# Scores of 24 expert chunks made ahead in the query and gate stages and kept in DRAM; the gathered tokens' slots chosen inside the first V group; six row places

## The chip, the cores and the metric

The kernel runs on one core of a Trainium2 chip. A core has five engines that run their own instruction queues and wait for each other with semaphores: PE (TensorE: matmuls), DVE (VectorE), ACT (ScalarE), POOL (GpSimd) and SP (SyncE, which here only starts DMAs). The metric is the time of one execution on the device, in microseconds; lower is better. The time before is the median of three runs.

## The reference

One step of a one-layer decoder: attention with a sliding window next to a gated linear recurrence, an output projection, and then the part that takes most of the time, a layer of 16,384 experts (PEER). For each of 576 tokens and each of 8 heads it finds the 16 best experts by two sets of 128 keys, and adds up their outputs:

```python
q = (hc @ w_pq).reshape(c, PEER_HEADS, 2, D_KEY // 2)
s = jnp.einsum('nhcd,hckd->nhck', q, sub_keys).astype(jnp.float32)
sv, si = lax.top_k(s, PEER_TOPK)
cand = (sv[:, :, 0, :, None] + sv[:, :, 1, None, :]).reshape(c, PEER_HEADS, -1)
cid = (si[:, :, 0, :, None] * N_KEYS + si[:, :, 1, None, :]).reshape(c, PEER_HEADS, -1)
best, pos = lax.top_k(cand, PEER_TOPK)
eid = jnp.take_along_axis(cid, pos, axis=-1)
g = jax.nn.softmax(best, axis=-1)
act = jax.nn.gelu(jnp.einsum('nd,nhkd->nhk', hc, peer_u[eid]).astype(jnp.float32))
return jnp.einsum('nhk,nhkd->nd', (g * act).astype(hc.dtype), peer_v[eid])
```

D_MODEL is 2048, PEER_HEADS 8, PEER_TOPK 16, N_KEYS 128; peer_u and peer_v are 16,384 x 2,048 in float32.

## The kernel before

**The tokens.** 416 tokens ("dense") go through all 16,384 experts: their scores against every row of u, times a gate that is zero for experts not chosen, times v. The other 160 tokens ("gathered") have the rows of their chosen experts fetched one by one with indirect DMAs. Both go on at once.

**Pieces.** Every weight comes in pieces of 256 KB: SP starts the load (`raw`), ACT copies it to `phi` (the high part, line 89), and DVE or POOL subtracts to get `plo` (the low part, line 90). `mm3` (lines 93 to 96) multiplies with three matmuls, high by high, high by low and low by high. The raw buffers are 3, and 4 more (`rawx`) once a pool is put into the list `deep`.

**Stages.** Projections, attention and recurrence, and the output projection (0 to 721 us of the trace). Then:
- *Query stage*: 8 heads. For each head PE makes the queries (`pdq` for the dense tokens and 32 of the others, `pgq` for 128 gathered tokens) and the scores `psc` against the keys; DVE and POOL choose the top 16 (`head_top`, `tile_ids`). The 128 gathered tokens' queries go to DRAM (`qgd`).
- *Gate stage* (lines 925 to 968): 13 groups of 32 tokens, 4 blocks of 8 each. DVE builds two one-hot factors `ohA` and `ohB`, PE multiplies them to the gates `pgg` of these tokens over all experts (8 matmuls in float32, 16 records in the trace), ACT copies them into `stg`, and SP writes the group to DRAM (`Gd`), since in SBUF there is no room for all.
- *Main loop*: 16 groups of 8 chunks, a chunk being 128 experts. `u_chunk` makes the scores of one chunk for the dense tokens (`sps`: 4 pieces, 48 matmuls of 416 columns), scales them and applies GELU (`e`). `w_chunk` multiplies `e` with the chunk's gates, read back from `Gd` (`gs`), and splits the product into `wth` and `wtl`. `v_group` multiplies a group's 8 weights with V: 16 output blocks `po` of 24 matmuls and two pieces each, which DVE adds into `acc`.
- *Gathered rows*: 640 jobs, each an indirect DMA of a half row of u or v (on POOL's queue, into one of four places `row`) and one DVE instruction on it. `pace` hands them out, so many for each "unit" (half a chunk or one output block), from unit 40 on. Before the first, `gather_top` has to choose the experts of the 128 gathered tokens: 8 heads of scores (`psg_`) and top 16, then the numbers.

**What sets the order.** The code is written in one order, and a scheduler orders each engine's queue by what it thinks is ready; it also moves work across stages as far as buffers allow. The scores of the first 8 chunks are kept in 8 buffers `ep`, so that chunks 0 to 4 run while DVE finishes the last head (the "tail") and chunks 5 to 7 are held by `g_late` until the last but one block of gates, to lie beside the way of the gates through DRAM (the "round trip"). `gather_top` stands between them and V group 0 in the code.

Of the kernel before, what the change touches and what calls it, by code (L numbers as in the profile page):

```python
# [35 lines left out]
EB = 8  # L36
# [3 lines left out]
UNIT0 = 40  # L40
# [4 lines left out]
def tile_hymba_peer_step(ctx: ExitStack, tc: tile.TileContext, a, o, dbg=None):  # L45
# [78 lines left out]
    Gd = gd_pool.tile([NSG, P, NGRP, 8, GRP], F32, name="Gd")  # L124

# [588 lines left out]
    def ffn_rstd():  # L714
# [104 lines left out]
    with tc.tile_pool(name="tq", bufs=1) as tq:  # L819
# [34 lines left out]

        for h in range(8):
# [42 lines left out]
    epx = ctx.enter_context(ExitStack())  # L898
    ep = [epx.enter_context(tc.tile_pool(name="ep", bufs=EB, side="right"))]


    psx = ctx.enter_context(tc.tile_pool(name="psx", bufs=2, space=PSUM))
    with tc.tile_pool(name="gb", bufs=1) as gbp, tc.tile_pool(name="psg", bufs=2, space=PSUM) as psg:
# [31 lines left out]

        nxt = prep(0)
        fac = factors(*nxt, 0)
        for r in range(NGRP):
# [8 lines left out]
            for q in range(GRP // BT):  # L947
# [25 lines left out]
    GT = ctx.enter_context(tc.tile_pool(name="gt", bufs=1))  # L973
# [6 lines left out]
    def row():  # L980
        return mn.tile([P, 1024], F32, tag="row", name="row", bufs=4)

    def gather_top():
# [25 lines left out]
        dve.tensor_scalar(idx2[:, 1], t1, 2.0, 1.0, op0=ALU.mult, op1=ALU.add)  # L1009

# [83 lines left out]
    es = {}  # L1094

    def u_chunk(c):

        sps = psx.tile([P, DEN], F32, name="sps")
        for q in range(4):
            held = EB - 3 <= c < 8  # L1100
            wh, wl, ins = piece(a["uT"][c, :, q * 4:q * 4 + 4], [P, 4, P], c < 8 and q % 2 == 1)
            with tc.issue_after(g_late.ins) if held else nullcontext():
                for d in range(4):
                    dk = q * 4 + d
                    mm3(sps, wh[:, d], wl[:, d], uh[dk][:, 0:DEN], ul[dk][:, 0:DEN], dk == 0, dk == NK - 1)
            if q % 2 == 1:
                pace(ins)
        e = ep[0].tile([P, DEN], F32, name="e")
        dve.tensor_tensor(e, sps, rd[:, 0:DEN], op=ALU.mult)
        act.activation(e, e, AF.Gelu_apprx_tanh)  # L1110
# [159 lines left out]
```

## Time and profile before

| what | us |
|---|---|
| median of three runs | 3446.27 |
| the three runs | 3442.35, 3447.62, 3446.27 |
| profiled execution, its own time | 3442.77 |
| its span in the trace | 3440.9 |
| query stage | 721 to 958 |
| tail | 958 to 1013 |
| gate stage | 1013 to 1151 |
| round trip | 1151 to 1202 |
| V groups and U chunks | 1202 to 3437 |

The stages' limits are read from the timeline of PE and DVE: 721 is the first `pdq`, 958 about where the last scores `psc` are done, 1013 the first `pgg`, 1151 the end of the last one, 1202 about the first `po`. A busy PE is one that works on a matmul; its clock can be lower than full, which the column PEclk tells (1.00 is full speed).

### The profile page before, as it was taken

Reading aid. Unit: us, or ns where it says so; the run is one execution under the profiler, and the core shown is the slowest. Engines: PE = TensorE matmul, PEld = TensorE weight load, DVE = VectorE, ACT = ScalarE, POOL = GpSimd, SP = SyncE. Lnnn points to the kernel's source line nnn. Section 1 sums busy time; section 2 is a strip of 40 time slices with the busy share of each in tenths; the row PEclk is TensorE's granted clock in tenths of the full one; section 3 lists DMA queues with packets and bytes.
Section 4 is the critical chain, followed back from the end, with each engine's and each line's share of the span. In section 5 each row is a group of like instructions: output and inputs, shape, how many; then the busy total and the mean of one; then the engine's idle time right before and its main releaser. Section 6 shows DMA issues by size and latency. Waiting matters only on the chain.

```text
span 3440.9 us, 52423 instructions
## 1 busy us (share of the span) xinstructions
PE 3358.9 (98%) x18611; PEld 3222.1 (94%) x18611; DVE 2550.5 (74%) x4765; ACT 1228.3 (36%) x2119; POOL 1200.3 (35%) x1174
## 2 busy tenths in 40 slices
PE   9999999999987899999999999999999999999999
PEld 7888888899887799999999999999999999999999
DVE  5386755446989777778787787877777778787786
ACT  4245533333233333333233332333333333333332
POOL 6562321124730123333333333333333333333331
PEclk9999999999999999999999999999999999999999
DMA  4211223433235647888888888888888888888886
GB/s 146 83 62 58 64 68 113 122 108 90 75 103 196 205 154 271 279 296 275 296 292 280 297 276 296 292 281 298 276 296 288 281 295 289 308 291 280 293 281 211
DMA packets 352774, 753.67 MB, mean 219 GB/s; under 512 B 39904, under 2 KB 104032, under 8 KB 352224
## 3 DMA queue, kind: packets, MB, share of 16 engines
q1 hardware_dynamic: 260352, 414.73, 35.4%
q0 software_dynamic: 92160, 335.59, 29.9%
q8 instruction: 147, 2.41, 0.3%
q14 instruction: 115, 0.94, 0.1%
HBM read 715.51 MB, written 36.59 MB: 219 GB/s over the span
## 4 chain that ended last, share of the span: by engine, by line
PE 84%; DVE 10%; POOL 2%; issue 1%; DMA 1%; ACT 1%; SPq 0%; POOLq 0%; ACTq 0%; DVEq 0%
PE po L96 11%; PE po L94 11%; PE po L95 11%; PE sps L94 11%; PE sps L95 11%; PE sps L96 11%; PE pd L96 2%; PE pd L95 2%; DVE ohA L952 2%; PE pd L94 2%; PE zp L94 1%; PE zp L95 1%; PE zp L96 1%; DVE ohB L954 1%; PE mm L94 1%
## 5 line engine op out<-in xcount | busy, mean ns | idle before, releaser
L89 ACT ACTIVATE phi<-raw 128x512 fp32r<-128x512 f32 x1200 | 757.0, 632 | 1693.8 <-PE po L95 747.1
L90 DVE TENSOR_TENSOR plo<-raw,phi 128x512 fp32r<-128x512 f32 x1132 | 796.6, 704 | 288.0 <-ACT phi L89 280.4
L96 PE MATMUL po<-wth,plo 128*128 128x416 f32 x2048 | 722.4, 353 | 0.6 <-DVE plo L90 0.6
L94 PE MATMUL po<-wth,phi 128*128 128x416 f32 x2048 | 717.7, 351 | 0.3 <-DVE acc L1137 0.3
L95 PE MATMUL po<-wtl,phi 128*128 128x416 f32 x2048 | 715.0, 349 | 0.0
L1013 POOL DMA_INDIRECT row<-in_u,idx x320 | 372.3, 1164 | 712.8 <-DVE au L1019 600.1
L1013 POOL DMA_INDIRECT row<-in_v,idx x320 | 383.5, 1198 | 669.9 <-DVE xg L1025 447.0
L96 PE MATMUL sps<-uha,plo 128*128 128x416 f32 x1536 | 538.0, 350 | 7.2 <-DVE plo L90 7.2
L94 PE MATMUL sps<-uha,phi 128*128 128x416 f32 x1536 | 537.7, 350 | 6.1 <-ACT phi L89 5.5
L95 PE MATMUL sps<-ula,phi 128*128 128x416 f32 x1536 | 537.2, 350 | 0.0
L95 PEld LDWEIGHTS po<-wtl,phi 128*128 128x128 f32 x2048 | 384.7, 188 | 5.9
L96 PEld LDWEIGHTS po<-wth,plo 128*128 128x128 f32 x2048 | 384.0, 188 | 3.4 <-DVE plo L90 0.9
L94 PEld LDWEIGHTS po<-wth,phi 128*128 128x128 f32 x2048 | 384.4, 188 | 2.8 <-DVE acc L1137 0.7
L1025 DVE SCALAR_TENSOR_TENSOR xg<-row,gg,xg 128x1024 f32<-128x1024 f32 x256 | 321.9, 1279 | 0.1
L1019 DVE CUSTOM_DVE_ANT_0 row<-row,hg 128x1024 f32<-128x1024 f32 x256 | 307.0, 1218 | 0.1
L96 PEld LDWEIGHTS sps<-uha,plo 128*128 128x128 f32 x1536 | 289.1, 188 | 9.3 <-DVE plo L90 9.2
L94 PEld LDWEIGHTS sps<-uha,phi 128*128 128x128 f32 x1536 | 289.1, 188 | 7.2 <-ACT phi L89 6.2
L95 PEld LDWEIGHTS sps<-ula,phi 128*128 128x128 f32 x1536 | 289.1, 188 | 0.1
L1137 DVE TENSOR_TENSOR acc<-po,acc 128x416 f32<-128x416 f32 x256 | 150.9, 590 | 182.9 <-PE po L96 182.8
L90 POOL TENSOR_TENSOR plo<-raw,phi 128x512 fp32r<-128x512 f32 x68 | 94.3, 1389 | 269.9 <-ACT phi L89 260.2
L96 PE MATMUL sps<-uhb,plo 128*128 128x416 f32 x512 | 180.2, 352 | 0.8 <-POOL plo L90 0.7
L94 PE MATMUL sps<-uhb,phi 128*128 128x416 f32 x512 | 180.2, 352 | 0.5 <-ACT phi L89 0.5
(427 smaller groups left out, 5401.2 us busy)
## 6 DMA issues: line engine op xcount, KB each, us to landing
raw<-in_uT SPq DMA_DIRECT2D x512, 256.0 KB
raw<-in_vL SPq DMA_DIRECT2D x512, 256.0 KB
Gd<-stg SPq DMA_DIRECT2D x13, 2048.0 KB
gs<-Gd SPq DMA_DIRECT2D x196, 128.0 KB
raw<-in_wlru SPq DMA_DIRECT2D x64, 256.0 KB
raw<-in_wout SPq DMA_DIRECT2D x64, 256.0 KB
raw<-in_wpq SPq DMA_DIRECT2D x64, 256.0 KB
raw<-in_wqkv SPq DMA_DIRECT2D x48, 256.0 KB
```

Source lines behind the costliest of these rows:

```text
L89: act.activation(hi, raw, AF.Copy)
L90: ins = (pool if on_pool else dve).tensor_tensor(lo, raw, hi.bitcast(F32), op=ALU.subtract)
L94: pe.matmul(out, lhsT=sh, rhs=mh, start=first, stop=False)
L95: pe.matmul(out, lhsT=sh, rhs=ml, start=False, stop=False)
L96: pe.matmul(out, lhsT=sl, rhs=mh, start=False, stop=last)
L952: dve.tensor_tensor(ohA, oa[:, q0, :, None].to_broadcast([P, BT, 16, 8]), ob[:, q0, None, :].to_broadcast([P, BT, 16, 8]), op=ALU.mult)
L954: dve.tensor_tensor(ohB, tT[:, 1, n0:n0 + BT, None].to_broadcast([P, BT, P]), iot[:, None, :].to_broadcast([P, BT, P]), op=ALU.is_equal)
L1013: pool.indirect_dma_start(out=r, out_offset=None, in_=uv[w], in_offset=bass.IndirectOffsetOnAxis(ap=idx2[:, half, e:e + 1], axis=0))
L1019: dve.tensor_tensor_reduce(r, r, rows[0][:, half * 1024:half * 1024 + 1024], 1.0, 0.0, ALU.mult, ALU.add, au[:, half, e:e + 1])
L1025: dve.scalar_tensor_tensor(xs, r, gg[:, e:e + 1], xs, op0=ALU.mult, op1=ALU.add)
L1137: dve.tensor_tensor(acc[:, b, 0:DEN], po, acc[:, b, 0:DEN], op=ALU.add)
```

## The change

- `u_chunk` becomes `u_parts`, a generator that makes a chunk's scores piece by piece. In the query stage one chunk follows each head (chunks 0 to 7; the odd pieces' `plo` on POOL). In the gate stage a generator `ahead` gives out the 64 pieces of chunks 8 to 23 evenly over the 52 blocks, all `plo` on DVE.
- The scores of chunks 0 to 39 go from SBUF to DRAM tiles `Ed` with a DMA on ACT's queue, and `w_chunk` reads them back with a DMA on SP's. `e` has three places. `g_late`, the held chunks and the pool `ep` are gone; the four `rawx` buffers are there from the query stage on.
- `gather_top` becomes a generator of eleven steps, one taken after each output block of V group 0. When it is done its pool is closed, and two more row places are opened (`rowx`, taken by every third fetch).
- Groups 0 to 3 make 4 chunks each instead of 8, the later ones 8. The first chunk after V group s is `done`, which starts at 24. Row jobs start at unit 20 and are spread over 464 units instead of from unit 40 over 512.

```diff
+NE = 24
+QE = 8
-UNIT0 = 40
+UNIT0 = 20
+UNITS = 256 + 2 * (128 - NE)
+    Ed = [gd_pool.tile([P, DEN], F32, name=f"Ed{c}") for c in range(NE + 16)]
+    def score_tile():
+        return per.tile([P, DQ], F32, tag="e", name="e", bufs=3)
-                sq = op.tile([P, DQ], F32, tag="sq", name="osq", bufs=2)
+                sq = score_tile()
+    def u_parts(c, place, split_on_pool):
+        sps = place()
+        for q in range(4):
+            wh, wl, ins = piece(a["uT"][c, :, q * 4:q * 4 + 4], [P, 4, P], split_on_pool and q % 2 == 1)
+            for d in range(4):
+                dk = q * 4 + d
+                mm3(sps, wh[:, d], wl[:, d], uh[dk][:, 0:DEN], ul[dk][:, 0:DEN], dk == 0, dk == NK - 1)
+            if c >= NE and q % 2 == 1:
+                pace(ins)
+            if q == 3:
+                e = score_tile()[:, 0:DEN]
+                dve.tensor_tensor(e, sps, rd[:, 0:DEN], op=ALU.mult)
+                act.activation(e, e, AF.Gelu_apprx_tanh)
+                if c < len(Ed):
+                    act.dma_start(Ed[c], e)
+                else:
+                    es[c] = e
+            yield
...
-            pd = [psm.tile([P, DQ], F32, tag="mm" if h % 2 == 0 else "pg" if c else "pt", name="pdq", bufs=1 if h % 2 and c else 2)
-                  for c in range(2)]
+            pd = [psm.tile([P, DQ], F32, tag="mm", name="pdq", bufs=2) for _ in range(2)]
...
+            for _ in u_parts(h, lambda: psm.tile([P, DEN], F32, tag="pg", name="sps"), True):
+                pass
...
+        ahead = (x for c in range(QE, NE) for x in u_parts(c, u_place, False))
+        nb, total, given = 0, NGRP * (GRP // BT), 0
...
-                if (r, q) == (NGRP - 1, 1):
-                    g_late = ins
                 act.activation(stg[:, :, q0], pg.rearrange("p n i -> p i n"), AF.Copy)
+                nb += 1
+                while given < nb * (NE - QE) * 4 // total:
+                    next(ahead)
+                    given += 1
...
     def row():
+        fetched[0] += 1
+        if more_rows and fetched[0] % 3 == 0:
+            return more_rows[0].tile([P, 1024], F32, tag="rowx", name="row", bufs=2)
         return mn.tile([P, 1024], F32, tag="row", name="row", bufs=4)
...
-        want = min(len(jobs), max(0, state[0] - UNIT0) * len(jobs) // (NSG * 32 - UNIT0 - 4) + 1)
+        want = min(len(jobs), max(0, state[0] - UNIT0) * len(jobs) // (UNITS - UNIT0 - 4) + 1)
...
     def w_chunk(c, gs):
-        e = es.pop(c)
+        e = es.pop(c, None)
+        if e is None:
+            e = score_tile()[:, 0:DEN]
+            sp.dma_start(e, Ed[c])
...
+            if s == 0:
+                next(top, None)
...
     gs = load_g(0)
-    W = []
-    for k in range(8):
-        u_chunk(k)
-        W.append(w_chunk(k, gs))
-    gather_top()
+    W = [w_chunk(k, gs) for k in range(8)]
+    top = gather_top()
+    done = NE
     for s in range(NSG):
         more = s < NSG - 1
         if more:
-            u_chunk(8 * s + 8)
+            u_chunk(done)
+            done += 1
         gs = v_group(s, W)
-        if more:
-            W = [w_chunk(8 * s + 8, gs)]
-            for k in range(1, 8):
-                u_chunk(8 * s + 8 + k)
-                W.append(w_chunk(8 * s + 8 + k, gs))
+        W = []
+        for k in range(8 if more else 0):
+            c = 8 * s + 8 + k
+            if done <= c or s < 4 and k in (2, 4, 6):
+                u_chunk(done)
+                done += 1
+            W.append(w_chunk(c, gs))
```

Below are PE's and SP's queues at three places, before and after. A row is a line of the code, the operation, what it writes and reads, its shape, and how many stand in a row; lines 94 to 96 before are 96 to 98 after.

PE before, where the last head's queries (`pdq`, `pgq`) and scores (`psc`) end and the first chunk's scores (`sps`) begin:

```order
L96 MATMUL pdq<-uhb,plo 128x448
L94 MATMUL pgq<-phi,ugh 128x256
L95 MATMUL pgq<-plo,ugh 128x256
L96 MATMUL pgq<-phi,ugl 128x256
L828 MATMUL psc<-skt,qTd 128x128 x4
L873 MATMUL ptq<-ident,qg 128x128 x2
L828 MATMUL psc<-skt,qTd 128x128 x2
L828 MATMUL psc<-skt,qTd 64x128 x4
L94 MATMUL sps<-uha,phi 128x416
```

PE after, at the scores of the last but one head:

```order
L96 MATMUL sps<-uha,phi 128x416
L97 MATMUL sps<-ula,phi 128x416
L857 MATMUL psc<-skt,qTd 128x128 x3
L902 MATMUL ptq<-ident,qg 128x128 x2
L857 MATMUL psc<-skt,qTd 128x128
L98 MATMUL sps<-uha,plo 128x416
L96 MATMUL sps<-uha,phi 128x416
```

The head's scores now stand in the middle of a chunk, so that matmuls of that chunk stand ahead of and behind them.

PE before in the gate stage, the blocks `pgg` and between them only the transposes `ptr` of the chosen numbers:

```order
L96 MATMUL sps<-uhb,plo 128x416
L961 MATMUL pgg<-ohA,ohB 128x128 x64
L909 MATMUL ptr<-ident,eg_6888 128x128 x3
L961 MATMUL pgg<-ohA,ohB 128x128 x128
L909 MATMUL ptr<-ident,eg_6889 128x128 x3
L961 MATMUL pgg<-ohA,ohB 128x128 x128
L913 MATMUL ptr<-ident,ei_5523 64x32 x6
L961 MATMUL pgg<-ohA,ohB 128x128 x80
L94 MATMUL sps<-uha,phi 128x416
```

PE after, at the stage's first blocks:

```order
L97 MATMUL sps<-ula,phi 128x416
L999 MATMUL pgg<-ohA,ohB 128x128 x16
L98 MATMUL sps<-uha,plo 128x416
L96 MATMUL sps<-uha,phi 128x416
L97 MATMUL sps<-ula,phi 128x416
L98 MATMUL sps<-uha,plo 128x416
```

Two blocks (16 matmuls) are now followed by score matmuls, 23 to 25 of them before the next two.

PE before at the last blocks of gates:

```order
L95 MATMUL sps<-ula,phi 128x416
L96 MATMUL sps<-uha,plo 128x416
L961 MATMUL pgg<-ohA,ohB 128x128 x16
L94 MATMUL sps<-uha,phi 128x416
L95 MATMUL sps<-ula,phi 128x416
L96 MATMUL sps<-uha,plo 128x416
```

PE after at the last blocks of gates (`po` is the first output block of V, `psg_` the first head of `gather_top`):

```order
L97 MATMUL sps<-ulb,phi 128x416
L98 MATMUL sps<-uhb,plo 128x416
L999 MATMUL pgg<-ohA,ohB 128x128 x32
L1044 MATMUL psg__12698<-row 128x128 x2
L96 MATMUL po<-wth,phi 128x416 x2
L97 MATMUL po<-wtl,phi 128x416
L98 MATMUL po<-wth,plo 128x416
```

The last four blocks now stand together, and V's first matmuls are next behind them; before, scores of chunks 5 to 8 stood there.

SP before at the same place, from the last write of gates to the first loads of `gather_top`:

```order
L966 DMA Gd<-stg 128x16x256
L77 DMA raw<-in_uT 128x512 x3
L1070 DMA gs<-Gd 128x1024 x3
L1070 DMA gs<-Gd 128x256
L993 DMA row<-qgd 128x256
L994 DMA row<-in_skT 128x256
L77 DMA raw<-in_uT 128x512 x5
```

SP after:

```order
L79 DMA raw<-in_vL 128x512 x2
L1006 DMA Gd<-stg 128x16x256
L1122 DMA gs<-Gd 128x1024 x3
L1122 DMA gs<-Gd 128x256
L1040 DMA row<-qgd 128x256
L1041 DMA row<-in_skT 128x256
L1150 DMA e<-Ed_75 128x416
L1150 DMA e<-Ed_76 128x416
L1150 DMA e<-Ed_77 128x416
```

The loads of V stand ahead of the last write of gates now, and the scores of chunks 3 to 5 are read behind the gates; those of chunks 0 to 2 are read earlier, into the three places.

## Rows read from the trace of the kernel before

**Rows 1.** The page's first part: span, then busy time of each engine, share, instructions.

```profile
span 3440.9 us, 52423 instructions
PE 3358.9 (98%) x18611; PEld 3222.1 (94%) x18611; DVE 2550.5 (74%) x4765; ACT 1228.3 (36%) x2119; POOL 1200.3 (35%) x1174
```

**Rows 2.** By stage: us, PE, PEld, DVE, ACT, POOL busy, PEclk, DMA share, GB/s.

```profile
721.00:958.00 237.00, 226.65 (x1341) 210.11 (x1339) 168.41 (x774) 74.73 (x147) 120.78 (x146) 0.99 0.29 87
958.00:1013.00 55.00, 48.44 (x241) 45.75 (x242) 52.90 (x189) 21.25 (x34) 27.69 (x32) 0.97 0.28 85
1013.00:1151.00 138.00, 110.19 (x877) 101.96 (x876) 132.82 (x149) 54.93 (x58) 4.15 (x2) 1.00 0.57 191
1151.00:1202.00 51.00, 39.65 (x193) 36.48 (x192) 35.28 (x134) 16.75 (x32) 10.54 (x12) 0.87 0.64 209
1202.00:3437.00 2235.00, 2234.10 (x11899) 2221.18 (x11898) 1752.11 (x2725) 755.87 (x1242) 776.37 (x665) 1.00 0.83 280
```

**Rows 3.** The same view, only sps: us, PE, PEld, DVE busy, PEclk, DMA, GB/s.

```profile
1013.00:1151.00 138.00, 5.07 (x27) 4.43 (x26) 0.58 (x1) 1.00 0.57 191
1151.00:1202.00 51.00, 35.75 (x169) 32.34 (x168) 1.76 (x3) 0.87 0.64 209
```

**Rows 4.** PE's timeline: start, us, engine, line, operation, out<-in, count, idle before.

```profile
1013.78 3.84 PE L961 MATMUL pgg<-ohA,ohB 128*128 128x128 f32 x32 [0.21 <-DVE ohA L952]
```

**Rows 5.** PE's waits in the query stage, the tail, the gate stage: us, times, longest.

```profile
PE pdq L96 <- POOL plo L90: 6.3, 5, 1.9
PE psc L828 <- ACT qTd L868: 1.8, 2, 1.6
...
PE sps L96 <- DVE plo L90: 5.5, 4, 2.3
...
PE pgg L961 <- DVE ohB L954: 13.5, 33, 1.3
PE pgg L961 <- ACT stg L965: 11.9, 11, 1.2
```

**Rows 6.** Groups by line: plo on POOL, busy us and mean ns, idle before.

```profile
L90 POOL TENSOR_TENSOR plo<-raw,phi 128x512 fp32r<-128x512 f32 x68 | 94.3, 1389 | 269.9 <-ACT phi L89 260.2 <-issue 9.2 <-POOL cand L767 0.2
```

**Rows 7.** DVE's timeline: a plo, and what starts behind it.

```profile
1214.72 0.68 DVE L90 TENSOR_TENSOR plo<-raw,phi 128x512 fp32r<-128x512 f32 x1
1215.32 0.08 DVE L755 MATCH_VALUE_LOAD row<-gg,s 128x8 f32 x1
```

**Rows 8.** DVE's timeline in the gate stage: an ohA, and the ohB behind it.

```profile
1034.92 1.22 DVE L952 TENSOR_TENSOR ohA<-oa,ob 128x1024 f32<-128x1024 f32 x1
1036.06 1.22 DVE L954 TENSOR_TENSOR ohB<-tT,iot 128x1024 f32<-128x1024 f32 x1
```

**Rows 9.** Timelines of ACT, SP and DVE at the round trip, in order of time.

```profile
1150.95 1.03 ACT L965 ACTIVATE stg<-pgg 128x1024 f32<-128x1024 f32 x1 [0.76 <-PE pgg L961]
...
1152.00 0.36 SPq L966 DMA_DIRECT2D Gd<-stg  x1
...
1161.03 1.75 SPq L1070 DMA_DIRECT2D gs<-Gd  x4
...
1168.13 3.60 DVE L1116 TENSOR_TENSOR e<-e,gs 128x416 f32<-128x416 f32 x7 [0.76 <-DMA gs<-Gd]
...
1185.92 0.33 SPq L77 DMA_DIRECT2D raw<-in_uT  x1
...
1189.16 1.67 ACT L89 ACTIVATE phi<-raw 128x512 fp32r<-128x512 f32 x3 [3.90 <-DMA raw<-in_uT]
```

**Rows 10.** Busy time by stretch, columns as in rows 2.

```profile
1160.00:1202.00 42.00, 30.64 (x145) 27.50 (x144) 33.37 (x131) 13.43 (x27) 9.25 (x11) 0.84 0.61 202
1202.00:1262.00 60.00, 59.41 (x318) 58.51 (x317) 53.46 (x183) 19.36 (x32) 22.91 (x28) 1.00 0.47 142
```

**Rows 11.** Groups by line: the DVE instruction of a row job.

```profile
L1019 DVE CUSTOM_DVE_ANT_0 row<-row,hg x256: 1210/1218/1228, 1302.7 to 2879.6; 128x1024 f32<-128x1024 f32 x128
```

**Rows 12.** Busy time by stretch, columns as in rows 2: 10 us, then 100 us.

```profile
1350.00:1360.00 10.00, 10.00 (x55) 9.91 (x54) 7.01 (x11) 2.60 (x5) 1.95 (x3) 1.00 1.05 394
2900.00:3000.00 100.00, 100.00 (x533) 99.37 (x533) 78.64 (x105) 32.60 (x53) 37.10 (x32) 1.00 0.89 303
```

More of the change, by code (lines that the diff above doesn't have):

```diff
@@ L35 @@
 QW = 1536
-EB = 8
+NE = 24
+QE = 8
 RAW = 3
@@ L729, in ffn_rstd @@
         opx.close()
+    es = {}
+    def u_parts(c, place, split_on_pool):
[16 more added lines that the diff above has]
+            yield
     qgd = gd_pool.tile([P, 16, P], F32, name="qgd")
@@ L853, in part_q @@
                     mm3(pg, ugh[:, kb], ugl[:, kb], wh[:, e], wl[:, e], kb == 0, kb == NK - 1)
+        deep.append(tq)
         for h in range(8):
@@ L897, in tile_hymba_peer_step, with u_place @@
     psx_.close()
-    epx = ctx.enter_context(ExitStack())
-    ep = [epx.enter_context(tc.tile_pool(name="ep", bufs=EB, side="right"))]
+    late = ctx.enter_context(tc.tile_pool(name="late", bufs=1, side="right"))
+    deep[0] = late
     psx = ctx.enter_context(tc.tile_pool(name="psx", bufs=2, space=PSUM))
+    def u_place():
+        return psx.tile([P, DEN], F32, name="sps")
     with tc.tile_pool(name="gb", bufs=1) as gbp, tc.tile_pool(name="psg", bufs=2, space=PSUM) as psg:
@@ L960, in tile_hymba_peer_step @@
                 for k in range(BT):
-                    ins = pe.matmul(pg[:, k], lhsT=ohB[:, k], rhs=ohA[:, k].rearrange("p a b -> p (a b)"),
-                                    start=True, stop=True)
-                if (r, q) == (NGRP - 1, 1):
-                    g_late = ins
+                    pe.matmul(pg[:, k], lhsT=ohB[:, k], rhs=ohA[:, k].rearrange("p a b -> p (a b)"),
+                              start=True, stop=True)
                 act.activation(stg[:, :, q0], pg.rearrange("p n i -> p i n"), AF.Copy)
+                nb += 1
+                while given < nb * (NE - QE) * 4 // total:
+                    next(ahead)
+                    given += 1
             sp.dma_start(Gd[:, :, r].rearrange("s p i n -> p s i n"),
@@ L972, in tile_hymba_peer_step @@
     pst = ctx.enter_context(tc.tile_pool(name="pst", bufs=1, space=PSUM))
-    GT = ctx.enter_context(tc.tile_pool(name="gt", bufs=1))
+    gtx = ctx.enter_context(ExitStack())
+    GT = gtx.enter_context(tc.tile_pool(name="gt", bufs=1))
+    more_rows = []
     uv = [a["u"].rearrange("e (t c) -> (e t) c", t=2), a["v"].rearrange("e (t c) -> (e t) c", t=2)]
@@ L980, in row @@
     def row():
+        fetched[0] += 1
+        if more_rows and fetched[0] % 3 == 0:
+            return more_rows[0].tile([P, 1024], F32, tag="rowx", name="row", bufs=2)
         return mn.tile([P, 1024], F32, tag="row", name="row", bufs=4)
+    fetched = [0]
     def gather_top():
@@ L999, in gather_top @@
             head_top(sc, P, si[:, 2 * h:2 * h + 2], gg[:, h * 16:h * 16 + 16], pos[:, h * 16:h * 16 + 16], GT, 1)
+            yield
         for hf in range(2):
@@ L1003, in gather_top @@
                      gg[:, q0:q0 + 64], GT)
+            yield
         t1 = r1[:, 768:768 + P + SPR]
@@ L1009, in gather_top @@
         dve.tensor_scalar(idx2[:, 1], t1, 2.0, 1.0, op0=ALU.mult, op1=ALU.add)
+        gtx.close()
+        more_rows.append(ctx.enter_context(tc.tile_pool(name="rx", bufs=1)))
+        yield
     def fetch(w, e, half):
@@ L1092, in tile_hymba_peer_step @@
     dve.tensor_reduce(sel, ident.rearrange("p (g n) -> p n g", n=SPR), axis=AX.X, op=ALU.add)
[L1094 to L1110, printed above, removed]
-        es[c] = e
     def w_chunk(c, gs):
-        e = es.pop(c)
+        e = es.pop(c, None)
+        if e is None:
+            e = score_tile()[:, 0:DEN]
+            sp.dma_start(e, Ed[c])
         ev = e.rearrange("p (g n) -> p g n", n=GRP)
@@ L1142, in v_group, with u_chunk @@
         return nxt
+    def u_chunk(c):
+        for _ in u_parts(c, u_place, False):
+            pass
     gs = load_g(0)
-    W = []
-    for k in range(8):
-        u_chunk(k)
-        W.append(w_chunk(k, gs))
-    gather_top()
-    epx.close()
-    late = ctx.enter_context(tc.tile_pool(name="late", bufs=3, side="right"))
-    ep[0] = late
-    deep.append(late)
+    W = [w_chunk(k, gs) for k in range(8)]
+    top = gather_top()
+    done = NE
     for s in range(NSG):
```

## The prediction

> **What bounds the kernel now.** I read the page's engine line first [rows 1]: TensorE (PE) is busy for 3358.9 of 3440.9 us. The change takes no matmul away and adds none, so it can only win time in which PE stands still or runs slow, and that is looked for stage by stage. The view that cuts the span at 721, 958, 1013, 1151 and 1202 us [rows 2] shows where: from 1202 us on PE is busy for 2234.1 of 2235 us with the clock at 1.00, so the main loop loses 0.9 us; before that, PE falls short in each of four stretches. The same row gives the price of a matmul on 416 columns: 2235 us / 11,899 = 0.188 us, so a U chunk (48 matmuls) costs 9.0 us and one output block of a V group (24) 4.5 us.
>
> The loss of each stretch, against the work that PE does in it:
> - Query stage, 721 to 958: 237 - 226.65 = 10.35 us idle, and 1% of clock, 2.3 us: 12.7.
> - Tail, 958 to 1013 (VectorE, DVE, finishes the last head's top-16 and the expert numbers): five U chunks, 45 us of work in 55: 10.1.
> - Gate stage, 1013 to 1151: two blocks take PE 3.84 us when it waits for nothing [rows 4], 1.92 each, 100 us for 52 blocks. With 5 us of U work [rows 3] and about 2 for the transposes that is 107 of 138: 31 lost. The waits name the cause: PE waits for the one-hot factor ohB, made on DVE, 33 times for 13.5 us, and for ACT's copy of the block [rows 5]. DVE is busy for 132.82 of 138 us [rows 2]: the stage is DVE's.
> - Round trip of the gates through DRAM, 1151 to 1202: 169 score matmuls [rows 3], 31.6 us of work, and some 3 for small products, in 51: 16.4. The clock is 0.87 here [rows 2].
>
> Sum: 12.7 + 10.1 + 31 + 16.4 + 0.9 = 71 us. That is all that the change can touch; the question is how much comes back.
>
> **The change part by part.**
>
> *Chunks 0 to 7 in the query stage.* The 8 x 9.0 = 72 us of PE work leave the tail and the round trip. In the order they stand between one head's query product and the next, so the waits there for ACT's copies (1.8 us for qTd among them) get cover. What stays: the waits for plo made on POOL, 6.3 us [rows 5]. POOL gets 16 more of these, 1.39 us each [rows 6], 22 us beside the 121 it has, over a stage that grows by 72: its share falls from 0.51 to 0.46. I take half of the plo waits and 1 us of clock: **4.5**.
>
> *Tail.* PE has 276 score matmuls queued there, 51.8 us. All 23 pieces of these now have plo on DVE, where 10 of 20 had: 13 more of 0.60 us each (one starts 0.60 us ahead of the next instruction [rows 7]), +7.8 on a DVE busy for 52.9 of 55 [rows 2], so 60.7 us until the first one-hot can follow, against 51.8. The end could be 8.9; the remainder of chunk 7 still lies behind the last scores and covers some of it: **6** (bounds 2 and 13, the latter if the 5.5 us that PE waits for plo here [rows 5] repeat).
>
> *Gate stage.* PE gets 12 chunks less the 36 matmuls done already, 101 us: 100 + 101 + 2 = 203 us. DVE has its 133 us, 45 plo of 0.60 (27) and 12 scalings of 0.51 (seven products of that size take 3.60 in [rows 9]; 6): 166. An ohA or ohB costs it 1.14 from start to start [rows 8]. So PE becomes the longer one by 37 us, and its queue holds 23 to 25 score matmuls (4.5 us) between two pairs of blocks, longer than one pair's factors on DVE (2.3 each). Loss **2** for edges (1 to 6).
>
> *Round trip.* The four last blocks stand back to back at the end of the stage, and behind them no score matmul is left; the next thing on PE's queue is the first output block, which needs the gate weights W. The chain [rows 9]: ACT's last copy 1.3 us after PE; the write to DRAM and its wait, from 1152.0 to the load's issue at 1161.0, 9.0; the load until the first product, 7.1. That makes 17.4. Then product, hi and lo part, some 0.6 each: 1.8, PE starts at 19.2. Only three scores wait in SBUF (three places "e"); the fourth needs a place, a load (3.2 us from issue to use in [rows 9]) and 1.8 again: 24.2, while PE has about 20 matmuls (3.8 us): 1.2 more; the same again at the seventh, 2.8 more. With 1.7 us for the clock that falls while PE stands (0.87 in this stretch before): **25**. Before, the same trip cost 16.4 because chunks 5 to 8 lay beside it. This is where the change pays: 8.6 us back. On SP's queue stand, behind the scores that wait for a place, gate loads and V loads; ten V loads are ahead of them, five blocks or 22 us of PE's work, so these are not late.
>
> *Choosing the gathered tokens' slots inside V group 0.* DVE's work for it: 33.4 + 53.5 us busy between 1160 and 1262 [rows 10], less 34 plo (20.4) and 32 instructions on 416 columns (16.4): 50. By the order 37 of it now stand between the first and the sixteenth accumulation, with 30 plo (18.0), 15 accumulations (7.7) and two more products (2): 65 us on DVE against 15 x 4.5 = 67.4 on PE. Before, DVE was busy for 53.5 of the 60 us after 1202 and PE for 59.4 [rows 10]. At 0.96 an engine that feeds plo in order will be late now and then; I take 5. Behind it come four chunks and one block, 40.6 us of PE, against 42 of DVE, since row jobs (1.22 us each [rows 11]) come in from unit 20 on: 2.5. In groups 1 to 3 the same stretch has 35.5 to 37.4 on DVE: 1 each. The loads of scores hide there: five that wait for a place, 5 us each with product and parts, beside 36 us of chunks; without these chunks 25 us would be open. Sum **10.5** (2 to 21).
>
> *Row places and the pace.* Six places instead of four let indirect loads start earlier; no wait of PE names them, so they bring nothing by themselves. Jobs per unit rise from 1.37 to 1.45 (640 over 440 and 468 units). From group 4 on DVE has some 118 us of work in a group of 144, 115 before: hidden. Score tiles through DRAM: 40 writes from ACT's queue, where only copies with slack stand behind them (ACT is busy for 54.9 of 138 in the gate stage [rows 2]), 40 loads on SP's. Transfers together: **2** (0 to 42, below).
>
> Sum after: 4.5 + 6 + 2 + 25 + 10.5 + 2 = 50 of 71 lost: **21 us gained**. The profiled execution took 3442.8 us (span 3440.9), so 3421.7; the median of the three runs is 3446.3, 3.5 above it, and on that scale the time is **3425**.
>
> **The rivals.**
> - *Full cover.* Tail 2, query 2, gate 1, the round trip 18 (no wait at score places), groups 2: 25 lost, 46 gained, **3400**. For it: DVE was at 0.89 with this same work after 1202 and PE lost 0.6 us. Against it: three score places and the 0.96 of group 0.
> - *Transfers become the bound (slower).* Groups 1 to 3 now do half the U work in the time of the same rows: V 8.4 MB, U 4.2, gates 1.7, scores read 1.7 and written 0.9, rows 24 units x 1.45 x 0.52 = 18.3: 35.1 MB in 16 x 4.51 + 4 x 9.02 = 108.2 us, 324 GB/s. From group 4 on 42.9 MB in 144.3, 297 (287 before). The highest 100 us stretch shows 303 at a share of 0.89 [rows 12]. If some 295 were what mixed transfers can do, groups 1 to 3 need 119 us, +10.8 each, and the eleven later ones +1.1: 44 us more than the forecast, **3469**. It decides from a limit below about 303. Against it: 10 us at 394 GB/s with PE busy for all ten [rows 12].
>  The Trainium skill (HBM Reference, Specifications) gives about 358 GB/s for each core where two share a memory and 425 for one alone; by that 324 fits, and the 394 of the trace stands above the first and below the second. The skill's Perfetto Trace Analysis, DMA Optimizations, says that transfers under 2 KB carry much overhead each; a score tile has 1,664 bytes per partition, so by this page the new traffic is of the costly kind; at the 240 GB/s of the gate load (1.70 MB in 7.1 us [rows 9]) in place of 324 its 2.6 MB would take 2.7 us more in each of groups 1 to 3, 8 us in all, and that only where transfers are the bound.
> - *New waits at the start of V.* Query 8, tail 13, gate 2, round trip 30, first groups 21: 74 lost against 71, **3449**, no change. For it: query, tail and first groups are near their upper bounds, and all hang on one thing, how closely plo on DVE follows PE. Against it: nowhere in these stages but the tail and group 0 is DVE's work within 10% of PE's.
>
> **How the numbers follow.** Forecast 0.53 (own range 3409 to 3440), full cover 0.17, transfers 0.13, new waits 0.17. 0.2%, about what a measurement can tell from no change here, is 7 us: 3439 to 3453 is "same". Faster: 0.50 of the forecast, 0.17, and 0.03 of the new waits: 0.70. Same: 0.03 + 0.11 = 0.14. Slower: 0.13 + 0.03 = 0.16. The range 3396 to 3453 leaves out the transfers, the rest of the new waits, and little else.
>
> **What would show it.** Right: the gate stage about 205 us long, PE over 0.95 busy in it, its waits for ohB nearly gone; behind the last block an idle stretch of 19 us ended by a W, larger than any before; PE in V group 0 with single waits for plo or po of a few us in all; from group 1 on PE 100% again. Wrong: PE idle in the gate stage for over 10 us; waits for raw loads in groups 1 to 3, or a longer period of U chunks there than 9.0 us (transfers); no idle stretch at the round trip (the scheduler's order isn't what is run).

## The result, and the profile after

The changed kernel takes **3418.7 us** (median of four runs, 3415.2 to 3422.5) against 3446.9 before: a ratio of 0.9919, 95% interval 0.9902 to 0.9936. 3425 was forecast, with 3396 to 3453 as the range. The profiled execution has a span of 3416.1 us; before it was 3440.9 [rows 1], so that 24.8 us are there to be explained from the two traces.

The page's first lines after:

```profile
span 3416.1 us, 52637 instructions
PE 3346.2 (98%) x18611; PEld 3213.7 (94%) x18611; DVE 2537.0 (74%) x4765; ACT 1236.6 (36%) x2127; POOL 1234.8 (36%) x1174
```

Busy time by stretch after, as in [rows 2] (us, PE, PEld, DVE, ACT, POOL busy, PEclk, DMA share, GB/s): query stage, tail, gate stage, round trip with V group 0, the stretch from there to the first accumulation of group 1, groups 2 and 3.

```profile
720.80:1027.60 306.80, 296.69 (x1721) 279.32 (x1719) 189.52 (x817) 106.96 (x191) 141.35 (x162) 0.99 0.34 102
1027.60:1083.60 56.00, 53.19 (x286) 52.07 (x283) 54.47 (x186) 26.48 (x42) 16.81 (x22) 1.00 0.40 126
1083.60:1280.38 196.78, 195.72 (x1389) 194.49 (x1387) 165.65 (x202) 86.86 (x112) 0.00 (x0) 1.00 0.65 208
1280.38:1381.40 101.02, 81.16 (x429) 78.74 (x430) 81.87 (x307) 31.48 (x55) 19.07 (x28) 0.92 0.54 171
1381.40:1434.49 53.09, 46.50 (x228) 44.84 (x227) 40.48 (x73) 18.67 (x31) 25.17 (x24) 0.92 0.91 336
...
1543.58:1653.61 110.03, 109.86 (x582) 108.18 (x581) 89.93 (x139) 37.05 (x62) 48.01 (x36) 1.00 0.93 328
1653.61:1764.88 111.27, 110.42 (x584) 108.67 (x582) 92.59 (x138) 36.75 (x62) 49.18 (x36) 1.00 0.93 326
```

The stages hold different amounts of U and V work now, so lengths can't be compared. I take the work out: from each stretch's length go 0.187 us for every score matmul and, from the round trip on, 0.189 for every matmul of V that the trace has in it. These prices come from DVE's timeline of before, where a chunk's scaling follows the last one by 8.98 us (48 matmuls) and an accumulation by 4.54 (24):

```profile
2016.77 0.59 DVE L1109 TENSOR_TENSOR e<-sps,rd 128x416 f32<-128x416 f32 x1 [1.02 <-PE sps L96]
2025.75 0.59 DVE L1109 TENSOR_TENSOR e<-sps,rd 128x416 f32<-128x416 f32 x1 [0.44 <-PE sps L96]
...
2079.72 0.59 DVE L1137 TENSOR_TENSOR acc<-po,acc 128x416 f32<-128x416 f32 x1 [1.05 <-PE po L96]
2084.26 0.59 DVE L1137 TENSOR_TENSOR acc<-po,acc 128x416 f32<-128x416 f32 x1 [1.10 <-PE po L96]
```

What is left is the stage's own work and its losses ("rest"). In the gate stage after, for example: 196.8 - 539 x 0.187 = 96.0.

| rest of the stretch, us | before | after | gain | forecast |
|---|---|---|---|---|
| query stage | 236.1 | 235.0 | 1.1 | 8.2 |
| tail | 11.3 | 4.0 | 7.3 | 4.1 |
| gate stage | 133.0 | 96.0 | 37.0 | 29 |
| round trip and V group 0 | 21.1 | 26.0 | -4.9 | -13.6 |
| up to the first accumulation of group 1 | -0.4 | 10.4 | -10.8 | -2.5 |
| groups 1 to 4 | -1.6 | 4.0 | -5.6 | -5 (with transfers) |
| after that | 3.7 | 4.0 | -0.3 | 0 |

The gains add up to 23.8; the query stage also starts 0.7 us earlier. So the gain comes from the gate stage above all, as forecast; four of the other rows are 3 to 9 us away from their forecasts. PE's waits after, from the query stage to group 1 (us in total, times, longest):

```profile
PE psg__12698 L1044 <- DMA row<-in_skT: 16.8, 1, 16.8
PE sps L98 <- DVE plo L92: 6.8, 5, 3.1
PE pdq L98 <- POOL plo L92: 4.6, 5, 2.4
PE po L96 <- ACT wth L69: 3.5, 1, 3.5
PE sps L98 <- POOL plo L92: 2.6, 2, 1.9
...
PE pgg L999 <- DVE ohB L992: 1.0, 2, 0.8
```

PE's waits for ohB fell from 13.5 us to 1.0, and those for ACT's copies from 11.9 [rows 5] to none: the gate stage is PE's. In their place stand 16.8 us at once, in the round trip (the wait is put down to a small load that came last; the rows below show that V's first weight was ready no earlier), and two waits behind V group 0, 3.1 us of the 6.8 for a `plo` and 3.5 for a `wth`. These two losses are the subject of the experiments, with the question of what the chunks in the query stage are worth.

The chain at the round trip, on SP, DVE, ACT and PE (start, us, operation, idle before):

```profile
1281.41 0.38 SPq L1006 DMA_DIRECT2D Gd<-stg  x1
...
1288.99 1.75 SPq L1122 DMA_DIRECT2D gs<-Gd  x4
...
1296.10 1.60 DVE L1152 TENSOR_TENSOR e<-e,gs 128x416 f32<-128x416 f32 x3 [6.42 <-DMA gs<-Gd]
...
1296.78 1.51 ACT L69 ACTIVATE wth<-e 128x416 fp32r<-128x416 f32 x3 [15.39 <-DVE e L1152]
...
1297.97 1.04 PE L96 MATMUL po<-wth,phi 128*128 128x416 f32 x2
```

The stretch behind V group 0 is read on DVE and POOL. POOL's timeline there (start, us, operation, idle before), then DVE's, then PE's two waits:

```profile
1388.69 1.18 POOL L1065 DMA_INDIRECT row<-in_u,idx  x1 [2.72 <-issue]
...
1395.16 0.94 POOL L1065 DMA_INDIRECT row<-in_u,idx  x1 [0.30 <-issue]
```

```profile
1387.52 0.24 DVE L1057 TENSOR_SCALAR idx<-row 128x160 uint32<-128x160 f32 x1
...
1388.93 0.68 DVE L92 TENSOR_TENSOR plo<-raw,phi 128x512 fp32r<-128x512 f32 x1
1396.59 1.23 DVE L1071 CUSTOM_DVE_ANT_0 row<-row,hg 128x1024 f32<-128x1024 f32 x1 [6.98 <-DMA row<-in_u,idx]
...
1397.74 0.69 DVE L92 TENSOR_TENSOR plo<-raw,phi 128x512 fp32r<-128x512 f32 x1
...
1428.10 1.22 DVE L1071 CUSTOM_DVE_ANT_0 row<-row,hg 128x1024 f32<-128x1024 f32 x1
...
1429.24 0.59 DVE L1152 TENSOR_TENSOR e<-e,gs 128x416 f32<-128x416 f32 x1
```

```profile
1398.48 0.46 PE L98 MATMUL sps<-uhb,plo 128*128 128x416 f32 x1 [3.09 <-DVE plo L92]
...
1430.47 1.06 PE L96 MATMUL po<-wth,phi 128*128 128x416 f32 x2 [3.50 <-ACT wth L69]
```

SP's load of the score for that second wait, and busy time while it was under way (us, PE, PEclk, DMA share, GB/s):

```profile
1414.78 0.38 SPq L1150 DMA_DIRECT2D e<-Ed  x1
```

```profile
1420.00:1430.00 10.00, 6.97 (x37) 0.99 1.04 397
```

The row numbers (idx) are written at 1387.5, POOL starts six fetches from 1388.7 on, and DVE, which comes to the first row's instruction right behind the plo of 1388.9, stands for 6.98 us until that row is there. The plo behind it comes at 1397.7, and PE has waited 3.09 us for it. Before the change the numbers were written at 1255.7, the first fetch started at 1256.9, and the first row was used only at 1302.7. The second wait is for the `wth` of a weight whose product `e` on DVE (1429.2) comes straight behind two row instructions. The score's load had been started at 1414.8, 14.5 us ahead of the product; the DMA engines were full while it was under way, and when it landed the trace does not show. So the order on DVE and the load itself are left as causes of this wait. The two waits are 6.6 of the 10.4 us; the clock, 0.92 in this stretch, goes with them.

### The profile page after: what moved, and what is told of

Same layout as the page of the kernel before. It is cut to its first block, busy times and chain, and to the rows that moved or that the text cites. A ratio compares the mean times of both kernels' runs of the same rounds, so it can differ in the third digit from the quotient of the medians.

```text
span 3416.1 us, 52637 instructions
## 1 busy us (share of the span) xinstructions
PE 3346.2 (98%) x18611; PEld 3213.7 (94%) x18611; DVE 2537.0 (74%) x4765; ACT 1236.6 (36%) x2127; POOL 1234.8 (36%) x1174
## 4 chain that ended last, share of the span: by engine, by line
PE 88%; DVE 6%; DMA 3%; POOL 1%; issue 1%; ACT 1%; SPq 0%; DVEq 0%; ACTq 0%; POOLq 0%
PE po L98 11%; PE po L96 11%; PE po L97 11%; PE sps L98 11%; PE sps L96 11%; PE sps L97 11%; PE pgg L999 3%; PE pd L98 1%; PE pd L97 1%; PE pd L96 1%; PE zp L96 1%; PE zp L97 1%; PE zp L98 1%; PE pdq L98 1%; PE mm L96 1%
## 5 line engine op out<-in xcount | busy, mean ns | idle before, releaser
L1065 POOL DMA_INDIRECT row<-in_v,idx x320 | 405.0, 1266 | 595.7 <-DVE xg L1077 366.8
L1065 POOL DMA_INDIRECT row<-in_u,idx x320 | 386.3, 1207 | 590.8 <-DVE au L1071 463.5
L97 PE MATMUL sps<-ulb,phi 128*128 128x416 f32 x512 | 180.3, 352 | 0.0
```

The source lines that it names most:

```text
L97: pe.matmul(out, lhsT=sh, rhs=ml, start=False, stop=False)
L1065: pool.indirect_dma_start(out=r, out_offset=None, in_=uv[w], in_offset=bass.IndirectOffsetOnAxis(ap=idx2[:, half, e:e + 1], axis=0))
```

## The experiments

Each kernel is the changed one with the edit shown. The rests of the stretches, worked out as above from each one's own trace:

| | query | tail | gate | round trip, V 0 | behind V 0 | group 1 | 2 | 3 | median, us |
|---|---|---|---|---|---|---|---|---|---|
| changed | 235.0 | 4.0 | 96.0 | 26.0 | 10.4 | 2.1 | 0.4 | 1.3 | 3418.7 |
| e1 gate only | 240.0 | 9.6 | 96.9 | 26.4 | 9.1 | 1.9 | 0.6 | -0.4 | 3429.1 |
| e5 the same, old places | 239.3 | 9.7 | 96.8 | 26.1 | 11.2 | 1.3 | 0.6 | -0.4 | 3427.9 |
| e2 query only | 235.4 | 33.4 | 135.4 | 26.8 | 4.9 | -0.4 | -0.4 | -0.4 | 3474.9 |
| e3 rows from unit 28 | 236.9 | 4.1 | 95.9 | 26.2 | -0.2 | 0.8 | 2.3 | 2.7 | 3412.8 |
| e4 two chunks held | 235.0 | 4.0 | 97.9 | 13.9 | 2.6 | 6.7 | 2.0 | -0.5 | 3408.1 |
| e6 e3 and e4 | 235.4 | 4.0 | 97.6 | 13.5 | 0.2 | 0.4 | 1.1 | 3.6 | 3404.2 |
| e7 top 16 written first | 235.4 | 4.1 | 95.9 | 25.4 | 11.8 | 0.5 | -0.4 | -0.4 | 3424.6 |
| e8 four row places | 235.5 | 4.1 | 95.9 | 25.7 | 4.8 | 1.3 | 1.5 | -0.4 | 3412.4 |
| e9 e6, four places | 237.0 | 4.1 | 97.9 | 14.5 | 0.2 | 1.2 | 1.4 | 2.5 | 3408.0 |

Executions of one of these kernels lie up to 11 us apart (e7: 3415.1 to 3425.8), and in the profiles the query stage, ahead of which nothing was changed, starts anywhere from 719.3 (e8) to 727.0 (e9). Differences of a few us between medians are therefore read in the rests and not in the times; the rests are those of one execution of each kernel.

**e1, chunks in the gate stage only.** NE = 16, QE = 0; the call in the loop over heads goes, and only groups 0 and 1 make four chunks.

```diff
-NE = 24
-QE = 8
+NE = 16
+QE = 0
...
-            for _ in u_parts(h, lambda: psm.tile([P, DEN], F32, tag="pg", name="sps"), True):
-                pass
...
-            if done <= c or s < 4 and k in (2, 4, 6):
+            if done <= c or s < 2 and k in (2, 4, 6):
```

> No chunks in the query stage, the same 16 in the gate stage (chunks 0 to 15); groups 0 and 1 make 4 chunks each, later ones 8. Theory (the gain is the gate stage's and the tail's; PE waits in the query stage for DVE and POOL, which are full there for three stretches, so chunks between the heads buy nothing): query stage about 237 us long, gate stage as in the changed kernel, time 3412 to 3421, as the changed kernel's 3418.7 or up to 5 us less, since fewer scores go through DRAM. Rival (the forecast's: chunks between the heads cover 8 us of waits): 3424 to 3430.

Measured: 3429.1 us (ratio to before 0.9950, 0.9934 to 0.9967), the rival's side. The gate stage is as in the changed kernel; the query stage is 5 us and the tail 5.6 us worse. My theory that the chunks between heads buy nothing fell. PE's longest wait in the query stage:

```profile
PE psc L857 <- ACT qTd L897: 8.0, 2, 4.5
```

The change also took away PSUM places: the query products `pdq` have one pair where they had two in turn. e5 gives them back.

**e5, the same with the old places.**

```diff
-            pd = [psm.tile([P, DQ], F32, tag="mm", name="pdq", bufs=2) for _ in range(2)]
+            pd = [psm.tile([P, DQ], F32, tag="mm" if h % 2 == 0 else "pg" if c else "pt", name="pdq", bufs=1 if h % 2 and c else 2)
+                  for c in range(2)]
```

> The first of these runs (no chunks in the query stage, 16 in the gate stage), with the PSUM places of the query products as they were before the change: two sets in turn in place of one. In that run PE waited 8.0 us at psc for ACT's copy qTd of a query product, since the next head's product had to wait for the same place. Theory (the chunk between two heads does no more than cover the place that it took): the stage falls from 240 to 236 us, psc's waits for qTd to 2, and the time from 3429 to 3423 to 3426; what is left against the changed kernel is the tail, 5.6 us. Rival (the chunk covers waits that were there before the change too): it stays at 3427 to 3431.

Measured: 3427.9 us (0.9951, 0.9934 to 0.9967). The waits for qTd fell as expected, the stage hardly did:

```profile
PE pdq L98 <- POOL plo L92: 8.6, 7, 1.9
...
PE psc L857 <- ACT qTd L898: 2.2, 2, 1.9
```

PE now waits for plo instead. So this stage without chunks keeps a rest of 239, and against it the chunks are worth some 4 us here and 5.7 in the tail; the rival held. The kernel before, with the same places and no chunks, had a rest of 236.1 in this stage and 6.3 us of waits for POOL's plo [rows 5]; what makes the stage 3 us longer in e5 stays open, so of the 4 us only 1 is a gain against before. In the tail DVE is busy for 60.77 of 66.2 us, where the changed kernel has 54.47 of 56.0 for nearly as much score work. What DVE carries into the tail from the query stage is a reading of these two rows that I did not test by itself.

```profile
960.30:1026.50 66.20, 62.44 (x310) 59.03 (x307) 60.77 (x211) 28.95 (x45) 17.43 (x23) 0.95 0.38 119
```

**e2, chunks in the query stage only.** NE = 8; all groups make eight chunks.

```diff
-NE = 24
+NE = 8
...
-            if done <= c or s < 4 and k in (2, 4, 6):
+            if done <= c:
```

> Chunks 0 to 7 in the query stage as changed, none in the gate stage; all groups make 8 chunks. Theory (gain from the gate stage and the tail): the tail has one chunk instead of five and loses some 35 us, the gate stage is DVE's again and loses 35, the way of the gates through DRAM stays at 20, boundaries lose little: 3465 to 3495, slower than before. Rival (the gain is the query stage's): 3435 to 3445.

Measured: 3474.9 us in a single run, as the theory had it. Tail and gate stage, and PE's longest wait in the tail:

```profile
1026.60:1069.00 42.40, 10.56 (x55) 9.36 (x51) 39.62 (x163) 6.34 (x13) 15.59 (x22) 0.65 0.19 56
1069.00:1204.38 135.38, 108.28 (x850) 99.93 (x850) 130.47 (x146) 53.09 (x54) 0.00 (x0) 0.98 0.56 187
```

```profile
PE pgg L999 <- DVE ohA L990: 26.7, 1, 26.7
```

Against the changed kernel the tail loses 29 and the gate stage 39. The chunks given out among the blocks of gates are where the gain is; the chunks in the query stage alone make the kernel slower than before, by more than any two runs of one kernel here differ.

**e3, row jobs from unit 28 on.**

```diff
-UNIT0 = 20
+UNIT0 = 28
```

> The changed kernel with UNIT0 28 for 20: row jobs begin inside V group 1 instead of between V group 0 and 1. Theory (after V group 0 DVE stands for 7 us in front of the first row job, whose row is just being fetched, with plo behind it, and six fetches at once fill the DMA engines): the stretch between the last accumulation of group 0 and the first of group 1 falls from 53 us to 42 to 46, time 3408 to 3413. Rival (the scores' way through DRAM and their three places hold that stretch): it stays at 51 to 54, time 3416 to 3421.

Measured: 3412.8 us (0.9903, 0.9886 to 0.9919). The stretch is 38.56 us long, and PE is busy for all of it (it also holds 21 matmuls of V less than in the changed kernel, 4 us, so that 42.5 is the length to compare):

```profile
1384.49:1423.05 38.56, 38.56 (x207) 38.17 (x207) 24.25 (x43) 17.57 (x30) 9.81 (x10) 1.00 0.77 267
```

```profile
1424.16 1.22 DVE L1071 CUSTOM_DVE_ANT_0 row<-row,hg 128x1024 f32<-128x1024 f32 x1
```

The same scores go through DRAM with the same three places, so these alone did not hold the stretch: the row jobs did. Six fetches still start at 1391.8, as soon as the numbers are there; the first of DVE's row instructions runs at 1424.2, over 30 us later and without a wait. But the edit takes all row instructions out of the stretch and not only the first (DVE is busy for 24.25 us in it, where the changed kernel has 40.48), and both of PE's waits there go. How much the first one cost is read from e8. Groups 2 and 3 lose 3 us more than in the changed kernel; the only longer waits of PE from there to the start of group 4, 1.6 and 2.5 us, are for an accumulation on DVE at the start of a group. Why DVE is late there I did not test.

**e8, four row places.**

```diff
-        if more_rows and fetched[0] % 3 == 0:
+        if no_rows and fetched[0] % 3 == 0:
```

(`no_rows` is an empty list.)

> The changed kernel with four row places in place of six. Theory (the places matter to PE only at the first fetches, where six at once fill the DMA engines): the stretch behind V group 0 gets 0 to 3 us shorter, groups 1 to 3 stay: 3415 to 3420. Rival (at 1.45 jobs per unit four places are too few, DVE waits for rows with plo behind them): groups from 1 on longer than 144.4 and 109 us, 3425 or more.

Measured: 3412.4 us (0.9911, 0.9895 to 0.9928), below the theory's span; the interval overlaps that of the changed kernel, so the times alone do not tell the two apart. The stretch behind V 0 has 5.6 us less rest, groups 1 to 3 no more. So the two more places bring nothing. The first row comes as late as with six (DVE idles 7.03 us for it, and POOL started on it 7.95 us before its use), and PE's wait for the plo behind it is the same:

```profile
1397.20 0.46 PE L98 MATMUL sps<-uhb,plo 128*128 128x416 f32 x1 [3.12 <-DVE plo L92]
```

What is gone is the second wait, the 3.5 us for a `wth`. So the first row's instruction costs at most the 4.8 us that are left here, and the other 5.6 of the changed kernel's 10.4 go with the second wait. With four places instead of six, the same score's load starts at 1412.0, its product comes 9.3 us later and not 14.5, behind one row instruction, and PE does not wait; the DMA engines are as full as with six from 1420 to 1430 (share 1.04), but moved 318 GB/s and not 399 between 1400 and 1410. Both the order on DVE and the transfers are left as causes; no run changed one of them by itself.

**e7, the top 16 written ahead of V group 0.**

```diff
     top = gather_top()
+    for _ in top:
+        pass
```

> The changed kernel with all eleven steps of gather_top written ahead of V group 0, as before the change, and nothing else moved. Theory (behind V group 0 the first row's fetch waits for the numbers, which are ready only at 1388 us, 108 us behind the last gates; before the change it was about 95): the numbers are ready 10 to 20 us earlier, the stretch from the last accumulation of group 0 to the first of group 1 falls from 53 to 42 to 48 us, V group 0 stays within 2 us: 3410 to 3415. Rival (DVE then has its top-16 work ahead of the first products of V, and V group 0 loses what the next stretch wins): 3416 to 3424.

Measured: 3424.6 us (0.9942, 0.9925 to 0.9959); its profiled execution is the fastest of its four, 3415.1. The numbers are ready 2 us earlier instead of 10 to 20, and DVE stands for 7.58 us:

```profile
1385.30 0.25 DVE L1057 TENSOR_SCALAR idx<-row 128x160 uint32<-128x160 f32 x1
...
1394.64 1.23 DVE L1071 CUSTOM_DVE_ANT_0 row<-row,hg 128x1024 f32<-128x1024 f32 x1 [7.58 <-DMA row<-in_u,idx]
```

My expectation fell: the place in the code does not set when the numbers come. The rival's time is nearer, but its mechanism is not there either (V group 0 loses nothing, and the next stretch wins nothing). PE has both waits again, 4.1 us for a plo and 3.5 for a wth. The median is 6 us above the changed kernel's, which the rests don't show; that stays open.

**e4, two chunks held behind the last gates.**

```diff
+            with tc.issue_after(hold.ins) if hold else nullcontext():
                 for d in range(4):
...
-        if more:
-            u_chunk(done)
+        for _ in range(2 if s == 0 else more):
+            u_chunk(done, None if s else g_last)
             done += 1
...
-            if done <= c or s < 4 and k in (2, 4, 6):
+            if done <= c or s < 4 and k in ((4, 6) if s == 0 else (2, 4, 6)):
```

(`g_last` is the last matmul of the gates.)

> The changed kernel with chunks 24 and 25 held until the last matmul of the gates, so that 96 score matmuls (18 us) stand between it and the first matmul of V; group 0 makes one chunk less behind it. Theory (the 17 us for which PE stands are the way of the gates through DRAM, and any work fills them): PE's idle time there falls from 17 to 3 or less; the last eight blocks of gates now stand together at DVE's pace, +3: time 3403 to 3409. Rival (the same stretch is late for another reason, the scores' loads or DVE; then V starts later by what PE does in between): 3415 to 3425.

Measured: 3408.1 us (0.9895, 0.9879 to 0.9912). PE's timeline around the last gates, where it waited:

```profile
1270.79 2.02 PE L1000 MATMUL pgg<-ohA,ohB 128*128 128x128 f32 x16 [0.25 <-DVE ohB L993]
...
1297.01 0.65 PE L96 MATMUL po<-wth,phi 128*128 128x416 f32 x2 [1.04 <-ACT wth L69]
```

In place of 16.8 us there are waits of about 1, and the rest of the stretch falls from 26.0 to 13.9. The gates' way through DRAM, from the last write to the first product, is about as long as in the other two (15.7 us; 16.1 before the change, 14.7 in the changed kernel); it had lost its cover. The gate stage costs 1.9 more. Behind V 0, PE waits 1.9 us in all for plo. Most of group 1's rest of 6.7 is one wait for a wth, at the first matmul of group 2:

```profile
1528.14 1.06 PE L96 MATMUL po<-wth,phi 128*128 128x416 f32 x2 [4.79 <-ACT wth L69]
```

So a wait of the second kind is there again, one group later; e6's rival expects this of the whole stall.

**e6, both.**

> Both remedies together: chunks 24 and 25 held behind the last gates, and row jobs from unit 28 on. Theory (the two losses, at the gates' way through DRAM and at the first row job, are independent): 3400 to 3404, that is the 10.6 us of the one and the 6.0 of the other off 3418.7. Rival (the stall behind V group 0 is one of scores coming late, and moves on to the next group): 3406 to 3410.

Measured: 3404.2 us (0.9884, 0.9868 to 0.9901; runs 3401.8 to 3407.5), just above the theory's numbers; the interval lies below the changed kernel's. The stretch behind V 0 and group 1 have rests of 0.2 and 0.4, and the wait for a wth of over 3 us is nowhere left, so the two losses are nearly independent: 14.5 us of the sum of 16.6 are won. Groups 2 to 4 keep 5 us more rest than in the changed kernel. This is the lowest median of the study, better than both kernels.

**e9, e6 with four row places.**

> Chunks 24 and 25 held behind the last gates, row jobs from unit 28 on, and four row places. Theory (six places cost time only where the first rows are fetched and used at once; with the later start that is gone): within 3 us of the same kernel with six places, 3400 to 3406, groups 1 to 3 no slower. Rival (six fetches in flight load the DMA engines in groups 1 to 3 as well): these groups get 3 to 5 us faster, 3397 to 3401.

Measured: 3408.0 us (0.9887, 0.9871 to 0.9904), 2 us above the theory's range and the same as e6 by the intervals; groups 1 to 3 have the same rest in sum (5.1 and 5.1). Without the early start the number of row places makes no difference that these runs show.

## Why the prediction was right, and where its steps were off

**Total.** 21 us of gain were forecast and 24.8 found between the profiles (28 between the medians). The steps agree less well than the sum, and that the sum came out is in part luck: the gate stage gave 8.0 more than forecast and the round trip with V group 0 lost 8.7 less, while the query stage gave 7.1 less and the stretch behind V group 0 lost 8.3 more. The sum also counts the main loop's 0.9 us as won, with no step behind it.

- **Gate stage, right and mis-sized.** That PE becomes the longer engine held: it is busy for 195.72 of 196.78 us, DVE for 165.65 (166 forecast). The stage gave 37 instead of 29, since I priced a pair of blocks by the length of a record, 3.84 us. From a pair's start to that of the next matmul it is 3.49 us, 91 us for 52 blocks and not 100. With the same 2 us for the transposes, 40 us had been lost before and not 31, and 3 are lost now. The prediction also set 4.5 us of score matmuls against "one pair's factors on DVE (2.3 each)"; 2.3 is the price of one block, and a pair's 4.6 fit only because PE's 3.49 us on the pair itself cover them too.

```profile
1083.58 3.73 PE L999 MATMUL pgg<-ohA,ohB 128*128 128x128 f32 x32
1087.07 0.43 PE L98 MATMUL sps<-uhb,plo 128*128 128x416 f32 x1
```

- **Tail, mis-sized.** DVE sets its end, as forecast (busy for 54.47 of 56.0 us), but has 54.5 us of work there and not 60.7. PE waits 1.6 us for plo, where it was 5.5 before. Where the 6 us went was not looked for.
- **Query stage, wrong step.** "I take half of the plo waits" had no row behind it but POOL's share over the whole stage. PE idles as long as before (10.1 us). The waits for ACT's copies went, as forecast; waits for plo, 10.1 in place of 7.2, took their place, and most of these, 7.2 us, are for plo made on POOL. A share over the stage does not show the queue at one moment: 4.0 us of the idle time lie between 880 and 920 us, where DVE is full with the numbers of several heads, and 2.8 between 920 and 940, where DVE is not and the plo stands on POOL behind that engine's own part of the numbers (`oh`):

```profile
880.00:900.00 20.00, 18.35 (x101) 16.54 (x100) 20.00 (x67) 4.84 (x11) 15.55 (x18) 1.00 0.26 66
900.00:920.00 20.00, 17.63 (x92) 16.57 (x92) 19.90 (x62) 6.54 (x13) 16.59 (x19) 0.91 0.26 73
920.00:940.00 20.00, 17.17 (x97) 15.59 (x97) 11.66 (x53) 4.86 (x8) 11.64 (x14) 1.00 0.33 105
```

```profile
924.95 3.13 POOL L829 TENSOR_TENSOR oh<-oh,sif 128x256 f32<-128x256 f32 x4 [0.69 <-DVE oh L826]
928.04 1.26 POOL L92 TENSOR_TENSOR plo<-raw,phi 128x512 fp32r<-128x512 f32 x1
...
929.35 0.68 PE L98 MATMUL pdq<-uha,plo 128*128 128x448 f32 x2 [2.35 <-POOL plo L92]
```

 The chunks are worth about 10 us all the same (e1, e5), against a kernel without them, in the tail more than here.
- **Round trip, right in its chain.** Last gate to first matmul of V: 17.6 us, 19.2 forecast (write and its wait 7.6 instead of 9.0, load 7.1 as read in [rows 9]). The waits for score places that I added, 1.2 and 2.8, are not there; in their place stand 0.4 us for a wtl and 2.3 in three waits for the loads of `gather_top`. e4 shows that the missing cover is what made PE stand.
- **V group 0, mis-sized.** DVE does reach 0.96 (65.11 of 68 us) and PE loses 1.65, not 5:

```profile
1308.00:1376.00 68.00, 66.35 (x357) 64.87 (x357) 65.11 (x260) 22.92 (x40) 14.82 (x23) 1.00 0.51 162
```

- **Behind V group 0, wrong step.** I compared sums of work (42 us on DVE against 40.6 on PE) and took 2.5. The sum says nothing on an instruction that stands at the head of DVE's queue for a row that is still under way, nor on a product that comes behind row instructions. The step failed where it took row jobs as 1.22 us each and left out the way of the first row and the order on DVE. e3 shows that the row jobs cause the loss; by e8 up to 4.8 us of it are the first row's, and the rest is a late weight, for which the order on DVE and full DMA engines are not told apart. That six places "bring nothing by themselves" was too good for them in this stretch, by the rests of e8.
- **The rivals.** Transfers: refuted as the bound of whole groups. Groups 2 and 3 move 328 and 326 GB/s, above the limit of 303 that this rival needed, and have rests of 0.4 and 1.3; the scores' trips through DRAM cost nothing that shows there. Behind V group 0, though, the DMA engines were full for some 30 us (share 1.04 at 397 GB/s from 1420 to 1430), and a part of them in the second wait is not ruled out. From group 5 on, the rest is that of before (4.0 and 3.7). Full cover was not reached in the changed kernel. New waits took 21 us back (4.9, 10.8 and 5.6 in the table), all from the round trip on; the forecast had 21.1 in the same three rows, divided otherwise, so this rival's 24 us more did not come. Against it the prediction held that DVE's work is within 10% of PE's only in the tail and group 0. Its own 42 against 40.6 behind V group 0 contradicts that, and two of the new waits came there (3.1 and 3.5 us). The HBM Reference, Specifications, in the Trainium skill gives a core about 358 GB/s when both cores of a memory stream and about 425 when it streams alone. By that the transfers had room, and the trace agrees for groups 2 and 3, by the figures above.

## What to carry to other kernels

Work that is moved into an engine's waits comes from somewhere: look at the place that it leaves, here a trip through DRAM that the same chunks had covered, and leave enough there. An instruction that consumes a transfer should stand in an engine's queue well behind the transfer's start; if it stands too early, the work queued behind it waits too, however small the sums of work look. A stage's loss is best measured by taking the known work out of its length, priced from start to start, since idle time and "busy" records each hide a part: PE's busy time fell by 12.7 us between the two kernels for the same 18,611 records.

## What the runs showed of the hardware

A row fetched with an indirect DMA was used 7.9 us after POOL started on its fetch (1388.69 to 1396.59), with six fetches started by then, and 7.95 us after it with four (e8). Over 53 us the core moved 336 GB/s. PE's granted clock was 0.92 over the two stretches in which it idled for 19.9 and 6.6 us; in e4, where chunks fill the first, it was 0.98 and 1.00 there.
